# Attention's values computed four heads at a time, one weight piece between key tiles, with the keys' norms tied to the last weight split

## The chip, the cores and the metric

One Trainium2 chip, one core. The metric is the device time of one execution in microseconds (us), the median over runs. Four engines do the work: TensorE (PE), VectorE (DVE), ScalarE (ACT) and GpSimd (POOL). SyncE (SP) issues the DMA transfers that matter here. PE's results land in PSUM, in slots that another engine must empty before they can be used again.

## The reference, cut to what matters

A decoder step of two layers, for 512 prompt tokens and 32 sample tokens at once (544 columns in all), with a width of 1024. After the first layer one shared set of keys and values is made, which is the only part that the change touches:

```python
def shared_kv(h, kv_norm, w_kvf, b_f, k_norm):
    xs = rmsnorm(h, kv_norm)
    kvf = xs @ w_kvf                      # 1024 -> 1024 keys, 1024 values, 8 forget values
    k = rmsnorm(kvf[..., :D_ATT].reshape(bsz, L, N_HEADS, HEAD_DIM), k_norm)
    v = kvf[..., D_ATT:2 * D_ATT].reshape(bsz, L, N_HEADS, HEAD_DIM)
```

There are 8 heads of 128. Keys are normed head by head, values are not. The second layer then begins with its first feed-forward block (called FFN2 here, since it is the second layer's), whose input is prepared while keys and values are still being computed.

## The kernel before, in words

**Precision.** Every fp32 matrix is split into a high part in the rounded matmul format and a low part, the rest. A product takes three matmuls: high by high, high by low, low by high (L241, L245, L247 for keys and feed-forward tiles; L798, L799, L800 for values).

**Weights.** They come in pieces of 128x1024 (512 KB). For each piece SP loads it (L165), ACT casts its high part (L198) and DVE subtracts for the low part (L199). Loads run four pieces ahead of the product that uses them and splits two pieces ahead (`prepare`). Each engine runs its program in order, so a cast or a split that stands behind other work on ACT or DVE comes late whenever that work does.

**A key or feed-forward tile** (`tile_mm`): one piece of weights, 8 blocks of 128 rows, each with three products in two column ranges of 256 and 288: 48 matmuls into one slot of the PSUM pool `ps` (three slots of 128x2x512).

**Keys.** A tile for each head. DVE multiplies the PSUM tile by the tokens' inverse norms (L762), ACT squares it (L708). For four heads at a time, a block of 8 small matmuls with ones sums the squares (L716), ACT and DVE turn the sums into inverse norms (L340 to L347), SP stores four rows (L727), and loads each back spread over 128 partitions (L732). DVE multiplies the key by its row (L860), and the normed key is stored and split (L861, L285, L286). Before the change that multiplication stands behind the last key product, `box["last"]` (L762), in DVE's program, by `issue_after`.

**Values.** Tokens stand on the partitions of the result, so the weights are the moving operand. `v_group` computes two heads at a time: it takes two pieces of weights at once, and for each of four blocks of 128 tokens runs 8 blocks of rows by three matmuls, each 256 columns wide, into a quarter of one `ps` slot. ACT then copies the four quarters out, scaled by the tokens' inverse norms (L804). Sample tokens get 8 small matmuls for each group from the raw weights (L809, into the pool `pb` with two slots of one bank), a scaled copy (L813), and, after the last group, two sums with a constant matrix (L850) that are copied out (L851). Each group's two heads are stored (L816), split (L285, L286) and stored again (L818).

**Beside it.** The input of FFN2 is prepared in pieces: `prep` (ACT L297, DVE L298) for each of 8 blocks and `forms` (ACT L307 and L285, DVE L311 to L314 and L286) for each pair. GpSimd runs a scan for the forget values (L899), and ACT and DVE a few operations on it (L908 and after).

**What sets the order.** `KV_ORDER` is a hand-written list that gives the order in which the steps are issued. A scheduler then places the instructions of each engine; its final order is what the rows below the diff show. Outside the stage of keys and values, the order is the same before and after the change.

## Time and profile before

| what | value |
|---|---|
| median of 3 runs | 2066.95 us (2066.77 to 2067.11) |
| the profiled execution's own time | 2067.01 us |
| its span in the trace | 2065.2 us |
| granted TensorE clock | 1.00 |
| PE busy | 2043.9 us, 99% of the span |
| DVE busy | 1507.2 us, 73% |
| ACT busy | 948.8 us, 46% |
| stage of keys and values: first value matmul | 999.86 us after the span's start |
| last value matmul | 1076.44 us |
| first matmul of FFN2 | 1078.48 us |

The profile is one execution. The span runs from its first to its last recorded work; the execution's own time has 1.8 us around that. Times of instructions are in us from the span's start. PE's rows overlap, since matmuls are pipelined: the cost of a matmul is read from the distance between the starts of consecutive ones, not from its duration.

### The profile page before, as it was taken

How to read it: one execution, taken by the hardware profiler on the slowest of the kernel's cores; microseconds unless marked ns; L12 is line 12 of the kernel's file. 1: busy time of each engine (PE TensorE's matmuls, PEld its weight loads, DVE VectorE, ACT ScalarE, POOL GpSimd, SP SyncE). 2: the span in 40 equal slices, each digit the busy share in tenths (PEclk: the TensorE clock that was granted, in tenths of full speed). 3: DMA queues.
4: the chain of work that ended last, by engine and by line, in shares of the span. 5: the costliest groups of instructions: out<-in, count | busy, mean ns of one | idle time of the engine just before them, and what ended most of it. 6: DMA issues, size and time to landing. Idle time of an engine off the chain costs nothing.

```text
span 2065.2 us, 38837 instructions
## 1 busy us (share of the span) xinstructions
PE 2043.9 (99%) x16432; PEld 2012.3 (97%) x16432; DVE 1507.2 (73%) x1866; ACT 948.8 (46%) x1404; POOL 186.2 (9%) x238
## 2 busy tenths in 40 slices
PE   8999999999999999999999999999999999999999
PEld 8999999999999999999999999999987999999999
DVE  7877777556687777776688777786476888777773
ACT  6535344423554344454356344444364654344451
POOL 0000000400100000043060000001142200000020
PEclk9999999999999999999999999999999999999999
DMA  5233234212223232432374332324668222232421
GB/s 184 84 110 109 73 107 144 94 44 83 83 92 113 72 110 77 151 98 82 115 261 156 105 101 95 113 68 127 208 205 302 102 99 86 100 101 84 131 95 44
DMA packets 93663, 237.95 MB, mean 115 GB/s; under 512 B 9506, under 2 KB 27202, under 8 KB 93490
## 3 DMA queue, kind: packets, MB, share of 16 engines
q1 hardware_dynamic: 93346, 235.44, 34.0%
q8 instruction: 129, 2.11, 0.4%
q14 instruction: 44, 0.36, 0.1%
q10 hardware_dynamic: 144, 0.04, 0.0%
HBM read 218.95 MB, written 16.49 MB: 114 GB/s over the span
## 4 chain that ended last, share of the span: by engine, by line
PE 92%; DVE 3%; ACT 2%; DMA 1%; issue 1%; POOL 0%; SPq 0%; ACTq 0%; DVEq 0%; POOLq 0%
PE ps L491 33%; PE ps L241 16%; PE ps L247 16%; PE ps L245 16%; PE pb L491 5%; DVE big L199 1%; PE ps L1234 1%; DMA tmp<-rows 1%; ACT big L198 1%; PE ps L1238 1%; PE ps L1237 1%; PE ps L1191 0%; DVE big L184 0%; PE ps L798 0%; ACT big L285 0%
## 5 line engine op out<-in xcount | busy, mean ns | idle before, releaser
L491 PE MATMUL ps<-big,big 128*128 128x272 f32 x5616 | 727.7, 288 | 1.7 <-DVE big L508 1.2
L491 PEld LDWEIGHTS ps<-big,big 128*128 128x128 f32 x5616 | 714.3, 188 | 2.3 <-issue 1.6
L199 DVE TENSOR_TENSOR big<-big,big 128x1024 fp32r<-128x1024 f32 (+2 forms) x538 | 592.1, 1103 | 106.7 <-ACT big L198 106.1
L198 ACT CAST big<-big 128x1024 fp32r<-128x1024 f32 (+2 forms) x538 | 487.9, 932 | 267.5 <-DVE big L184 262.7
L241 PE MATMUL ps<-big,big 128*128 128x256 f32 (+1 forms) x2704 | 563.0, 289 | 7.4 <-ACT big L198 7.4
L247 PE MATMUL ps<-big,big 128*128 128x256 f32 (+1 forms) x2704 | 558.7, 288 | 1.3 <-DVE big L199 1.3
L245 PE MATMUL ps<-big,big 128*128 128x256 f32 (+1 forms) x2704 | 558.1, 287 | 0.0
L241 PEld LDWEIGHTS ps<-big,big 128*128 128x128 f32 x2704 | 433.9, 189 | 10.9 <-ACT big L198 7.7
L245 PEld LDWEIGHTS ps<-big,big 128*128 128x128 f32 x2704 | 435.9, 189 | 0.0
L247 PEld LDWEIGHTS ps<-big,big 128*128 128x128 f32 x2704 | 433.1, 188 | 2.9 <-DVE big L199 2.5
L326 POOL TENSOR_TENSOR st<-st,tmp 128x544 f32<-128x544 f32 (+1 forms) x63 | 87.4, 1387 | 1590.6 <-ACT tmp L324 1590.5
L530 DVE SCALAR_TENSOR_TENSOR big<-ps,big 128x544 f32<-128x544 f32 x160 | 115.5, 722 | 106.5 <-PE ps L247 106.4
L184 DVE TENSOR_TENSOR big<-big,big 128x1024 f32<-128x1024 f32 x156 | 190.0, 1218 | 0.0
L499 ACT COPY tmp<-ps 128x544 f32<-128x544 f32 x117 | 71.7, 613 | 141.4 <-PE ps L491 141.4
L454 ACT ACTIVATE big<-big 128x544 f32<-128x544 f32 x88 | 58.0, 660 | 163.2 <-DVE big L451 162.0
L491 PE MATMUL pb<-big,big 128*128 128x272 f32 x936 | 124.0, 288 | 0.0
L451 DVE TENSOR_TENSOR big<-big,st 128x1088 f32<-128x1088 f32 x88 | 113.3, 1290 | 10.6 <-ACT big L513 8.9
L491 PEld LDWEIGHTS pb<-big,big 128*128 128x128 f32 x936 | 120.2, 188 | 0.0
L297 ACT ACTIVATE big<-big,gains 128x544 fp32r<-128x544 f32 (+1 forms) x80 | 55.8, 704 | 118.8 <-DVE big L530 64.9
L286 DVE TENSOR_TENSOR big<-big,big 128x544 fp32r<-128x544 f32 (+1 forms) x112 | 80.9, 728 | 36.3 <-ACT big L285 36.2
L298 DVE SCALAR_TENSOR_TENSOR big<-big,gains,big 128x544 fp32r<-128x544 f32 (+1 forms) x80 | 65.9, 832 | 26.5 <-ACT big L297 26.5
L285 ACT CAST big<-big 128x544 fp32r<-128x544 f32 (+1 forms) x112 | 71.3, 643 | 16.8 <-DVE big L457 8.9
(200 smaller groups left out, 1418.8 us busy)
## 6 DMA issues: line engine op xcount, KB each, us to landing
big<-in_w SPq DMA_DIRECT2D x156, 512.0 KB
big<-in_w2a SPq DMA_DIRECT2D x64, 512.0 KB
big<-in_w2b SPq DMA_DIRECT2D x32, 384.0 KB
big<-in_w13p SPq DMA_DIRECT2D x16, 512.0 KB
big<-in_win SPq DMA_DIRECT2D x16, 512.0 KB
big<-in_wg SPq DMA_DIRECT2D x16, 512.0 KB
big<-in_ck SPq DMA_DIRECT2D x16, 512.0 KB
big<-in_cv SPq DMA_DIRECT2D x16, 512.0 KB
```

The costliest lines, as they stand in the source:

```text
L184: self.nc.vector.tensor_tensor(t, a, b, ALU.add if op == "+" else ALU.subtract)
L198: self.nc.scalar.copy(hi, src)
L199: self.nc.vector.tensor_tensor(lo, src, hi.bitcast(F32), ALU.subtract)
L241: i = nc.tensor.matmul(out[:, a:b], wh, xh[:, a:b], start=s, stop=False)
L245: nc.tensor.matmul(out[:, a:b], wh, xl[:, a:b], start=False, stop=False)
L247: nc.tensor.matmul(out[:, a:b], wl, xh[:, a:b], start=False, stop=e)
L286: self.nc.vector.tensor_tensor(pair[:, 1, cols], src, pair[:, 0, cols].bitcast(F32), ALU.subtract)
L326: nc.gpsimd.tensor_tensor(acc[:, cols], acc[:, cols], sq, ALU.add)
L451: tt(g, g, rstd.unsqueeze(1).broadcast_to([P, 2, T]), ALU.mult)
L491: nc.tensor.matmul(dst[w], a[:, c], b, start=k in "152" and kp == 0 and n == 0, stop=kp == NKP - 1 and n == 2, skip_group_check=True)
L499: nc.scalar.copy(t["r" + k], t["C" if k == "5" else "A"])
L530: nc.vector.scalar_tensor_tensor(h[c], whole(out), 0.5, h[c], ALU.mult, ALU.add)
```

## The change

The values are computed in 8 steps of one piece of weights each. `_moving` lays the pieces out on the host so that one holds 512 columns (four heads) of two blocks of rows. Four steps make a half of the heads; two `ps` slots are held through the four steps (`half["p"]`), one for each pair of token blocks. A step has 24 matmuls of 512 columns. The sample tokens' products follow steps 1 and 3 of a half, four at a time, 512 columns wide. After the fourth step ACT empties both slots with 8 copies of 128x256 (now L829) and the sample's slot with one (L832). The step `w` stores and splits two heads; a half has two of them. The order list is written anew; value steps now stand between the later key tiles, so the weights' order changes too. Key norms stand behind `last_lo`, the last weight split (L199) that had been issued on DVE, where they stood behind the last key product.

The core of the diff (long unchanged or merely renamed parts left out; `columns`, `raw_sample` and `sample_sums` are the former inner code as methods):

```diff
-:k0|:k1|c|:k2|:k3|v0:,s0,,r0 r1|:k4 n0 r2|:k5 n1 r3|:k6 n2|:k7 n3|v1:,s1,p0,r4 r5 p1|v2:n4 p2,r6,n5 p3 f0,r7 p4|v3:n6 p5 f1,n7,p6,p7
+k0 k1 c0 k2 k3 k4 s0 k5 r0 r1 v0 k6 n0 r2 k7 n1 r3 p0 v1 n2 s1 p1 v2 n3 p2 v3 r4 r5 p3 f0 v4 n4 r6 w0 p4
+v5 n5 r7 w0 p5 v6 n6 f1 p6 v7 n7 p7 w0 w0
...
-        self.nc.vector.tensor_tensor(lo, src, hi.bitcast(F32), ALU.subtract)
+        self.last_lo = self.nc.vector.tensor_tensor(lo, src, hi.bitcast(F32), ALU.subtract)
...
+    def token_half(self, xs, xraw, half, u):
+        nc = self.nc
+        hi, lo = self.unit()
+        raw = self.raws[self.pieces[self.p_next - 1]["src"][0]]
+        self.advance()
+        if u == 0:
+            half["p"] = self.ps(), self.ps()
+            half["r"] = []
+        half["r"] += [raw[:, 0:512], raw[:, 512:1024]]
+        for i in range(4):
+            t, out = slice(i * P, i * P + P), half["p"][i // 2][:, i % 2, :]
+            for a in range(2):
+                k, c = 2 * u + a, slice(512 * a, 512 * a + 512)
+                xh, xl = xs[k]
+                nc.tensor.matmul(out, xh[:, t], hi[:, c], start=k == 0, stop=False)
+                nc.tensor.matmul(out, xh[:, t], lo[:, c], start=False, stop=False)
+                nc.tensor.matmul(out, xl[:, t], hi[:, c], start=False, stop=k == NC_ - 1)
+        if u % 2:
+            if u == 1:
+                half["s"] = self.pb()
+            for n in range(4):
+                k = 2 * u - 2 + n
+                nc.tensor.matmul(half["s"][32 * n:32 * n + 32, :], xraw[:, k, :], half["r"][k], start=k < 4, stop=k >= 4,
+                                 skip_group_check=True)
...
-        def v_group(g, beside):
+        def v_step(n):
+            g, u = divmod(n, 4)
+            self.token_half(xs, xraw, half, u)
+            if u < 3:
+                return
             rc = box["rc"]
...
+            vs = [self.flat(1024).rearrange("p (h i d) -> p h i d", h=2, i=4) for _ in range(2)]
             for i in range(4):
...
+                for a in range(2):
+                    nc.scalar.activation(
+                        vs[a][:, :, i], half["p"][i // 2][:, i % 2, 256 * a:256 * a + 256].rearrange(
+                            "p (h d) -> p h d", h=2), AF.Copy, scale=rc[:, i:i + 1])
+            nc.scalar.activation(sv[:, 512 * g:512 * g + 512], half["s"], AF.Copy, scale=rc[:, 4:5])
...
+        def v_store(_):
+            for hh, x in box["v"][:2]:
+                pair = self.big(F32R)
+                nc.sync.dma_start(out=o["v"][hh], in_=x)
                 self.split_pair(pair, x, slice(0, SEQ))
+                nc.sync.dma_start(out=self.vd[hh], in_=pair[:, :, :SEQ].bitcast(F32))
...
         def norm(hh):
-            with self.tc.issue_after(box["last"].ins):
+            with self.tc.issue_after(self.last_lo.ins):
                 self.k_norm(hh, kraw, rows)
...
+def _moving(w):
+    return w.reshape(4, 2, P, -1, 512).transpose(3, 0, 2, 1, 4).reshape(-1, P, 1024)
...
-    a["wv"] = w_kvf[:, D:2 * D].reshape(2, 4, P, 4, 256).transpose(3, 0, 2, 1, 4).reshape(8, P, 1024)
+    a["wk"], a["wv"] = _stationary(w_kvf[:, :D]), _moving(w_kvf[:, D:2 * D])
```

How the rows of the engines' programs move is shown at three places. In the names, a buffer is its pool and a number; `ps_12037` is the PSUM slot of before's last value group, `ps_11746` and `ps_11747` are the two of after's second half, and the line numbers of after are its own (L603 to L605 for L798 to L800, L611 for L809, L617 for L850, L829 for L804, L832 for L813, L868 for L851).

PE's program of before where the values end:

```order
L798 MATMUL ps_12037<-big_11845,big_10841 128x256
L799 MATMUL ps_12037<-big_11846,big_10841 128x256
L800 MATMUL ps_12037<-big_11845,big_10841 128x256
L809 MATMUL pb_12203<-big_11670,xraw 32x256 x4
L809 MATMUL pb_12203<-big_11676,xraw 32x256 x4
L850 MATMUL pb_12224<-big_11362,consts 32x512
L241 MATMUL ps_12253<-big_11781,big_12025 128x256
L241 MATMUL ps_12253<-big_11781,big_12025 128x288
```

PE's program of after, between the sixth and the seventh of the eight value steps:

```order
L605 MATMUL ps_11747<-big_11664,big_10601 128x512
L611 MATMUL pb_11828<-big_11472,xraw 32x512 x2
L611 MATMUL pb_11828<-big_11554,xraw 32x512 x2
L611 MATMUL pb_11828<-big_11625,xraw 32x512 x2
L611 MATMUL pb_11828<-big_11668,xraw 32x512 x2
L617 MATMUL pb_12012<-big_10940,consts 32x512
L603 MATMUL ps_11746<-big_11733,big_10700 128x512
L603 MATMUL ps_11747<-big_11733,big_10700 128x512
L617 MATMUL pb_12015<-big_10940,consts 32x512
L604 MATMUL ps_11746<-big_11734,big_10700 128x512
```

The sample's products of the last heads and their two sums stood between the last value matmul and FFN2 (the second sum inside FFN2's first tile). They now stand ahead of the last 46 value matmuls, and FFN2's first tile follows the last value matmul directly.

ACT's program of before around the third group's sample copy (L813), which PE's products of that group release:

```order
L198 CAST big_11845<-big_11676 128x1024
L285 CAST big_11887<-big_11431 128x512
L297 ACTIVATE big_11891<-big_87,gains 128x544
L285 CAST big_11951<-big_11431 128x512
L297 ACTIVATE big_11955<-big_87,gains 128x544
L307 ACTIVATE big_11958<-big_86,gains 128x544 x2
L813 ACTIVATE big_11362<-pb_12005,sm_11082 128x256
L285 CAST big_11963<-tmp_11961 128x544
```

ACT's program of after around the second half's sample copy (L832):

```order
L198 CAST big_11733<-big_11625 128x1024
L832 ACTIVATE big_10940<-pb_11828,sm_11083 128x512
L285 CAST big_11775<-big_11263 128x512
L285 CAST big_11781<-big_11701 128x512
L285 CAST big_11786<-big_11701 128x512
L297 ACTIVATE big_11791<-big_88,gains 128x544
L198 CAST big_11794<-big_11668 128x1024
L285 CAST big_11836<-big_11263 128x512
L285 CAST big_11842<-big_11702 128x512
L285 CAST big_11847<-big_11702 128x512
L297 ACTIVATE big_11852<-big_88,gains 128x544
L198 CAST big_11855<-big_11737 128x1024
```

Of before, the copy stands behind casts and preparations that belong to earlier work. Of after, it stands ahead of the casts of the first half's heads (`big_11701`, `big_11702`) and of the casts of three weight pieces, which all wait in ACT's program until PE has done that sample block.

ACT's program of before from the last group's copies to the weight cast of FFN2's third tile (`big_12247`):

```order
L804 ACTIVATE big_12038<-ps_12037,sm_11082 128x2x128 x4
L285 CAST big_12213<-big_12038 128x512
L285 CAST big_12218<-big_12038 128x512
L851 COPY big_12223<-pb_12224 32x512
L851 COPY big_12223<-pb_12227 32x512
L307 ACTIVATE big_12233<-big_88,gains 128x544 x2
L285 CAST big_12238<-tmp_12236 128x544
L285 CAST big_12239<-tmp_12237 128x544
L198 CAST big_12247<-big_12029 128x1024
```

ACT's program of after at the same place, from behind the eight copies L829 to the weight cast of FFN2's third tile (`big_12035`):

```order
L285 CAST big_11984<-big_11455 128x512
L297 ACTIVATE big_11988<-big_89,gains 128x544
L285 CAST big_11991<-big_11970 128x512
L285 CAST big_11996<-big_11970 128x512
L285 CAST big_12001<-big_11971 128x512
L285 CAST big_12006<-big_11971 128x512
L868 COPY big_12011<-pb_12012 32x512
L868 COPY big_12011<-pb_12015 32x512
L307 ACTIVATE big_12021<-big_88,gains 128x544 x2
L285 CAST big_12026<-tmp_12024 128x544
L285 CAST big_12027<-tmp_12025 128x544
L198 CAST big_12035<-big_11859 128x1024
```

Where four copies and two casts of heads stood ahead of the rest, eight copies, four casts of heads, the cast of the last key and one more preparation now stand.

More of the change, by code (lines that the diff above doesn't have):

```diff
@@ L565, in next_norm, with raw_sample, columns, sample_sums @@
         return on_chunk, box
+    def raw_sample(self, h, gcol, x):
+        for c in range(NC_):
+            self.nc.gpsimd.tensor_scalar(x[:, c, :], h[c][:, SEQ:], self.gain(gcol + c), None, ALU.mult)
+        return x
+    def columns(self, rstd):
+        nc, t = self.nc, self.pb()
+        for j in range(4):
+            nc.tensor.matmul(t[:, j:j + 1], rstd[:, j * P:(j + 1) * P], self.ident[:, 0:1], start=True, stop=True)
+        for j in range(4):
+            nc.tensor.matmul(t[32 * j:32 * j + 32, 4:5], rstd[:, SEQ:], self.ident[:, 0:1], start=True, stop=True,
+                             skip_group_check=True)
+        rc = self.sm(5)
+        nc.scalar.copy(rc, t[:, 0:5])
+        return rc
+    def token_half(self, xs, xraw, half, u):
[21 more added lines that the diff above has]
+                nc.tensor.matmul(half["s"][32 * n:32 * n + 32, :], xraw[:, k, :], half["r"][k], start=k < 4, stop=k >= 4,
+                                 skip_group_check=True)
+    def sample_sums(self, sv, half):
+        t = self.pb()[:NS, :]
+        self.nc.tensor.matmul(t, self.c[:, C_SUM:C_SUM + NS], sv[:, 512 * half:512 * half + 512], start=True, stop=True)
+        return t
     def pairs(self, box):
@@ L750, in kv @@
         nxt = {"x": {}, "f": []}
-        box = {}
+        box, half, sv = {}, {}, self.flat(1024)
         xraw = self.small.tile([P, NC_ * NS], F32, tag="xraw", name="xraw", bufs=1)[:].rearrange("p (c t) -> p c t", t=NS)
-        for c in range(NC_):
-            nc.gpsimd.tensor_scalar(xraw[:, c, :], h[c][:, SEQ:], self.gain(G_KV + c), None, ALU.mult)
+        self.raw_sample(h, G_KV, xraw)
         def k_tile(hh):
@@ L831, in prep, with forms @@
             nxt["x"][c] = self.prep(h[c], ffn_gain + c)
-        def forms(_):
-            nxt["f"].append(self.forms(h, ffn_gain, len(nxt["f"]), self.pairs(nxt)))
-        do = dict(k=k_tile, s=stats, r=row, n=norm, p=prep, f=forms)
-        parse = lambda s: [[lambda x=x: do[x[0]](int(x[1])) for x in y.split()] for y in s.split(",")]
-        for step in KV_ORDER:
-            head, _, rest = step.partition(":")
-            if head == "c":
-                columns()
-            elif head:
-                v_group(int(head[1]), parse(rest))
-            else:
-                for run in parse(rest)[0]:
-                    run()
+        def forms(n):
+            nxt["f"].append(self.forms(h, ffn_gain, n, self.pairs(nxt)))
+        do = dict(k=k_tile, v=v_step, w=v_store, c=cols, s=stats, r=row, n=norm, p=prep, f=forms)
+        for step in KV_ORDER.split():
+            do[step[0]](int(step[1:]))
         vs = self.big()[:NS, :, :512]
         for a in range(2):
-            t = self.pb()
-            nc.tensor.matmul(t[:NS, :], self.c[:, C_SUM:C_SUM + NS], box["sv"][:, 512 * a:512 * a + 512], start=True, stop=True)
-            nc.scalar.copy(vs[:, a, :], t[:NS, :])
+            nc.scalar.copy(vs[:, a, :], self.sample_sums(sv, a))
         nc.sync.dma_start(out=o["vs"].rearrange("t (a n) -> t a n", a=2), in_=vs)
@@ L1285, in build @@
         ple_units(0)
-        plain([i["wf"]] + [i["wk"][c] for c in range(4)] + [i["wv"][c] for c in range(2)])
-        plain([i["wk"][c] for c in range(4, 8)] + [i["wv"][c] for c in range(2, 8)])
+        plain([i["wf"]] + [i["w" + x[0]][int(x[1])] for x in KV_ORDER.split() if x[0] in "kv"])
         self.ffn_pieces(2)
```

51 lines of the change are left out of this document (5 added, 46 removed).

## The prediction

> **What bounds the kernel now.** I read the page first: busy times, then the chain of work that ended last.
>
> ```profile
> PE 2043.9 (99%) x16432; PEld 2012.3 (97%) x16432; DVE 1507.2 (73%) x1866; ACT 948.8 (46%) x1404; POOL 186.2 (9%) x238
> PE 92%; DVE 3%; ACT 2%; DMA 1%; issue 1%; POOL 0%; SPq 0%; ACTq 0%; DVEq 0%; POOLq 0%
> ```
>
> TensorE is busy 99% of the span and holds 92% of the chain. So the change can act in two ways only: by PE work that goes or comes, and by waits of PE that go or come. Then I cut the stage of the values out by windows. The columns are the stretch, its length, busy time and count of PE, weight loads, DVE, ACT and POOL, granted clock, DMA share and GB/s.
>
> ```profile
> 999.86:1076.44 76.58, 76.58 (x658) 72.31 (x656) 60.40 (x78) 35.93 (x60) 34.16 (x35) 1.00 0.64 219
> 1076.44:1105.20 28.76, 28.00 (x217) 25.23 (x216) 23.53 (x32) 21.40 (x35) 0.30 (x1) 1.00 0.81 281
> ```
>
> From the first value matmul to the last, PE never stops: 76.58 of 76.58. Nothing can be won there but PE's own work. After it PE is short by some 0.8 us, and ACT, at 21.40 of 28.76, and DVE, at 23.53, are far busier than their averages over the span: the preparation of FFN2 piles up here. PE's timeline shows where it stops.
>
> ```profile
> 1076.64 1.07 PE L809 MATMUL pb<-big,xraw 128*32 128x256 f32 x16
> 1077.53 1.02 PE L850 MATMUL pb<-big,consts 128*32 128x512 f32 x2
> 1078.48 0.52 PE L241 MATMUL ps<-big,big 128*128 128x256 f32 x2
> ...
> 1091.77 0.41 PE L241 MATMUL ps<-big,big 128*128 128x256 f32 x2
> ...
> 1092.72 0.52 PE L247 MATMUL ps<-big,big 128*128 128x256 f32 x2 [0.30 <-DVE big L199]
> ...
> 1098.57 0.42 PE L245 MATMUL ps<-big,big 128*128 128x256 f32 x2
> 1099.45 0.52 PE L247 MATMUL ps<-big,big 128*128 128x256 f32 x2 [0.46 <-DVE big L199]
> ```
>
> FFN2 begins at 1078.48; I call that moment P0. Its third tile begins at 1091.77, 13.3 us later. Of that, 1.1 is the second sum (0.95 from 1077.53 to 1078.48 for the first one, and 0.1 for entering), so a tile takes (13.3 - 1.1)/2 = 6.1. Pairs of one line follow at 0.25, so L247 of the third tile was due at 1091.77 + 0.50 = 1092.27 and came at 1092.72: 0.45 late, on DVE's split. In the fourth tile it was due at 1098.57 + 0.25 and came 0.63 late. Together 1.1 us: that is all that PE waits there now.
>
> **Part one: PE's own work.** The value matmuls of before and, from the attention of the second layer, a train of 512-wide ones:
>
> ```profile
> 999.86 0.28 PE L798 MATMUL ps<-big,big 128*128 128x256 f32 x1
> ...
> 1005.45 0.28 PE L800 MATMUL ps<-big,big 128*128 128x256 f32 x1
> ...
> 1509.84 0.39 PE L1076 MATMUL ps<-big,big 128*128 128x512 f32 x1
> ...
> 1510.54 0.28 PE L1082 MATMUL ps<-neg,identr 128*128 128x256 f32 x1
> ```
>
> From 999.86 to 1005.45 lie 47 steps: 0.119 us for a matmul of 256 columns, 384 x 0.119 = 45.7 us. From 1509.84 to 1510.54 lie three of 512 columns: 0.233 each, 192 x 0.2325 = 44.6. Halving the number and doubling the width saves 1.1 us and no more, since the columns set the time.
>
> One rule speaks against that size. The Trainium skill, "TensorE: Matmul & The Clock Gate", section "Back-to-back issue gap", gives about 131 ns as the sustained spacing of 512-wide matmuls; by it the 192 would take an estimated 25.2 us. The trace's 0.233 does not agree, and it decides.
>
> Sample products: four blocks now, each 1.00 from the rows below plus 0.2 for entering and leaving, 4.8 us.
>
> ```profile
> 1012.62 1.07 PE L809 MATMUL pb<-big,xraw 128*32 128x256 f32 x16
> 1013.62 0.52 PE L241 MATMUL ps<-big,big 128*128 128x256 f32 x2
> ...
> 1039.47 0.65 PE L716 MATMUL pb<-tmp,ones 128*32 128x272 f32 x2
> 1040.05 0.39 PE L799 MATMUL ps<-big,big 128*128 128x256 f32 x1
> ...
> 1044.41 1.12 PE L716 MATMUL pb<-tmp,ones 128*32 128x272 f32 x14
> 1045.46 0.39 PE L798 MATMUL ps<-big,big 128*128 128x256 f32 x1
> ```
>
> After, there are two blocks of twice the width: 2 x (2.00 + 0.2) = 4.4, so -0.4 (between 0, if entering doubles too, and -0.6). The second statistics (L716) stood as one matmul alone and seven together: 0.58 + 1.05 and twice the entering, 1.8. After, two stand inside the sample block and three times some stand between value matmuls: 2 x 0.07 + 2 x 0.68 + 1.0 = 2.5, so +0.7 (0 to +1). The two sums only move. Net: -1.1 - 0.4 + 0.7 = -0.8, and with the ends of these terms -1.7 to 0. I take -1.1, nearer the good end, since the long trains of 512 also spare entries that I have not counted.
>
> The second sum now waits for the sample's copy (L832), with 1.1 of the first sum and two value matmuls, 0.5, between. The copy is 0.6 by the casts of the same size below, so I cost it at nothing; if ACT comes to it late, each us past 1.6 is a us of PE.
>
> **Part two: what ACT and DVE owe FFN2.** This is the term that decides. Groups of ACT's instructions, from 1057 to 1100 (busy us and mean ns after the bar), then a window of ACT alone, then its timeline and DVE's split:
>
> ```profile
> L198 ACT CAST big<-big 128x1024 fp32r<-128x1024 f32 x6 | 6.1, 1045 | 0.0
> L307 ACT ACTIVATE big<-big,gains 128x544 f32<-128x544 f32 x8 | 5.5, 737 | 0.0
> L285 ACT CAST big<-tmp 128x544 fp32r<-128x544 f32 x8 | 5.2, 648 | 6.5 <-DVE tmp L311 5.2 <-DVE tmp L314 1.3
> L285 ACT CAST big<-big 128x512 fp32r<-128x512 f32 x8 | 4.8, 618 | 2.4 <-DVE big L860 2.2
> L297 ACT ACTIVATE big<-big,gains 128x544 fp32r<-128x544 f32 x6 | 4.4, 745 | 0.0
> L804 ACT ACTIVATE big<-ps,sm 128x256 f32<-128x256 f32 x8 | 3.1, 463 | 0.0
> ```
> ```profile
> 1057.50:1083.10 25.60, 18.11 (x30) 1.00 0.96 337
> ```
> ```profile
> 1083.11 1.54 ACT L804 ACTIVATE big<-ps,sm 128x256 f32<-128x256 f32 x4
> ...
> 1090.37 1.05 ACT L198 CAST big<-big 128x1024 fp32r<-128x1024 f32 x1
> ```
> ```profile
> 1091.44 1.23 DVE L199 TENSOR_TENSOR big<-big,big 128x1024 fp32r<-128x1024 f32 x1 [0.23 <-ACT big L198]
> ```
>
> Prices, busy over count: weight cast 1.02, L307 0.69, cast of a form 0.65, cast of a head 0.60, L297 0.73, value copy 0.39.
>
> Before, ACT reached the last value copies at 1083.11, ended the third tile's cast at 1091.42, and so took 8.3 us from the one to the other. After, in that piece of ACT's program stand four more value copies (+1.56), three more casts of heads or keys (+1.8) and one more L297 (+0.73): 8.3 + 4.1 = 12.4.
>
> When does ACT reach it? Its program holds the second half's sample copy ahead of everything else that is due, and PE reaches the end of that sample block 48 value matmuls and two sums before P0: 48 x 0.2325 + 2.2 = 13.4 us. From there to the value copies stand one copy (0.6), seven casts of heads and keys (4.2), three L297 (2.2), three weight casts (3.06), two L307 (1.38) and two casts of forms (1.3): 12.7 us of work. ACT works hand in hand with DVE there, so it waits. In the like stretch of before it was busy 18.11 of 25.60, 71%; without some 2 us that DVE lost beside GpSimd's scan, which after comes earlier, 77%. So 12.7 takes 16.5 to 17.9, and the value copies begin at P0 + 3.1 to P0 + 4.5. The third tile's cast ends at P0 + 15.5 to P0 + 16.9. The third tile is wanted at P0 + 12.2, two tiles after P0, as the sums no longer stand between. It starts 3.3 to 4.7 late, and L247 waits for DVE's split (1.23, of which the first two lines cover 0.5) another 0.7: 4.0 to 5.4. Without any wait of ACT the cast ends at P0 + 11.7 and only L247 is some 0.2 late. Between these ends I take 4.2, close to the rows with waits, on their lower side as ACT has less to ask of DVE while its own list is longer. The fourth tile keeps its 0.6. So PE waits 4.8 where it waited 1.1: **+3.7**.
>
> **Parts that I cost at nothing.** The keys move between value steps; their products are the same number. Weights come in another order, but still four pieces ahead, under a DMA share of 0.64 in the stage. Norms behind `last_lo`: the order on DVE then is split first, norm second, so a late row no longer holds that split; the cover is two pieces ahead, and what it costs if that is gone is the rival on rows below.
>
> **Sum**, against the profiled execution's 2067.01 (0.06 above the median, which changes nothing): 2067.0 - 1.1 + 3.7 = **2069.6 us**. That is slower by 0.13%; a measurement of this kernel can tell about 0.2%, 4.1 us, from no change.
>
> **The rivals.**
>
> *ACT keeps up.* If ACT and DVE hardly wait for each other, PE's stalls come to 0.2 + 0.6 = 0.8 for 1.1 now: 2067.0 - 1.1 - 0.3 = 2065.6. For it: ACT has only 25 us of work from the sample copy to the cast, in 25.6. Against it: in the two stretches quoted ACT was busy 71% and 74%.
>
> *Rows of the last keys land late* (the side of slower). The second statistics' rows are stored, loaded back, and used by a multiplication on DVE, behind which weight splits stand. Before:
>
> ```profile
> 1051.53 1.12 SPq L727 DMA_DIRECT2D rows<-st  x4
> 1053.08 0.84 SPq L816 DMA_DIRECT2D out_v<-big  x2
> ```
> ```profile
> 1059.00 1.31 DVE L860 SCALAR_TENSOR_TENSOR big<-big,gains,tmp 128x544 f32<-128x544 f32 x1 [0.42 <-DMA tmp<-rows]
> ```
>
> From the end of the statistics (1045.46) to the row in use (1059.00) 13.5 us went by, 7.5 of them in stores, loads and queue. After, the last statistics stand 31 value matmuls, the sample block, the sums and 48 value matmuls ahead of P0: 7.2 + 2.2 + 2.2 + 11.2 = 22.8. The last value step, wanted at P0 - 5.6, has its split on DVE behind the first such multiplication, three splits of heads and a few more, 1.3 + 3 x 0.65 + 1.4 + 1.2 = 5.9. So a row may land 11.3 us after the statistics; each us beyond is one of PE's. Four stores of values (1 MB) now stand directly ahead of the rows in SP's queue where two stood between store and load. With the 13.5 of before PE loses 2.2 more in the value steps: 2071.8. For it: that row. Against it: 6.1 of the 13.5 were DVE's own queue, beside a scan that is earlier now.
>
> *PSUM.* A half holds two of three `ps` slots, so a key tile inside it must use the third, and the next key tile waits until DVE has emptied it. If DVE is 4 us behind there, this costs some 3.5 us: 2073. Against it: only one key tile stands inside a half's steps after the first, and PE's windows show DVE busy 60 of 77.
>
> *The width costs nothing.* If a matmul cost 0.119 whatever its width, 192 x 0.119 = 22.8 would go: 2067.0 - 22.8 + 3.7 = 2048. The 0.233 of L1076 speaks against it. By the 131 ns of the Trainium skill's page "TensorE: Matmul & The Clock Gate", section "Back-to-back issue gap", it would be an estimated 2050.
>
> *The change doesn't save at all.* If the new trains break at each block as short ones do, the saving of 1.1 is nil: 2070.7; this lies within the forecast's own spread.
>
> **How the numbers follow.** Forecast with its spread (2068.6 to 2070.8): 0.56. ACT keeps up: 0.18. Rows late: 0.16. PSUM: 0.05. Width free: 0.02. The rest, 0.03, is something unseen, either way. The low end is the case in which ACT keeps up, 2065.4; the high end, 2072.7, takes in late rows with 0.9 us over. Faster by over 0.2% (below 2062.8): the width rival and half of the unseen, with a little of ACT keeping up and PE saving more, 0.06. Slower by over 0.2% (above 2071.1): late rows, PSUM and a little more, 0.22. Within: 0.72.
>
> **What would show it.** Right: in the profile after, 512-wide value matmuls at 0.233; the third FFN2 tile's first product waiting some 3.5 us for ACT's weight cast, that cast ending near P0 + 16, ACT's value copies starting near P0 + 4; nothing else of PE's waits in the stage. Wrong: a spacing far from 0.233; ACT's copies starting at P0 or before, or the third tile on time; PE waiting inside the value steps on a weight split (rows late: DVE's multiplication waits for the DMA) or on DVE's key product (PSUM).

## The result, and the profile after

The kernel after takes 2071.60 us (median of 13 runs, 2070.17 to 2072.89) where the kernel before, run beside it, takes 2066.77 (13 runs). The ratio is 1.0026, with a 95% interval of 1.0019 to 1.0033: slower by about a quarter of a per cent. The forecast was 2069.6, within 2065.4 to 2072.7. The profiled execution took 2071.60, 4.6 us more than the one of before. Of the experiments below, three executions in a slow state (3202.8 us of e1_old_tie, 2841.93 of e6_gpsimd_cast, 4049.92 of e10_values_earlier) are left out of the medians and ratios, while one of 2087.45 us of e8_late_cast is in them and lifts its ratio to 1.0034, where the medians alone give 1.0026.

The page of after, the engines' busy times:

```profile
PE 2044.9 (99%) x16208; PEld 2003.2 (97%) x16208; DVE 1507.3 (73%) x1866; ACT 948.2 (46%) x1402; POOL 181.4 (9%) x238
```

PE has 224 matmuls fewer (192 of the values and 32 of the sample, half the number at twice the width), and yet it is busy 1 us longer. Windows of after, from the first value matmul to FFN2, from there to FFN2's first matmul of the next kind (L491), and a piece of the latter (columns as in the prediction; the granted clock stands third from the end):

```profile
1012.38:1077.62 65.24, 65.24 (x343) 49.73 (x341) 53.64 (x69) 28.27 (x46) 28.78 (x34) 1.00 0.59 200
1077.62:1109.77 32.15, 27.86 (x194) 26.90 (x193) 24.88 (x33) 23.83 (x39) 0.21 (x1) 0.89 0.92 334
1094.57:1101.17 6.60, 6.60 (x28) 6.29 (x28) 5.83 (x8) 6.28 (x9) 0.00 (x0) 0.50 0.97 313
```

In the value steps PE never waits, as before. Behind them it stands still for 4.3 us, and for 6.6 us of its work the clock is granted at 0.50. PE's timeline of after shows the order of events:

```profile
1075.07 0.40 PE L604 MATMUL ps<-big,big 128*128 128x512 f32 x1
...
1077.38 0.40 PE L605 MATMUL ps<-big,big 128*128 128x512 f32 x1
1077.62 0.41 PE L241 MATMUL ps<-big,big 128*128 128x256 f32 x2
...
1082.77 0.52 PE L245 MATMUL ps<-big,big 128*128 128x256 f32 x2 [0.26 <-DVE big L298]
1083.13 0.41 PE L247 MATMUL ps<-big,big 128*128 128x256 f32 x2
1084.35 0.52 PE L241 MATMUL ps<-big,big 128*128 128x256 f32 x2 [0.82 <-ACT big L829]
...
1090.95 0.41 PE L247 MATMUL ps<-big,big 128*128 128x256 f32 x2
1094.57 0.82 PE L241 MATMUL ps<-big,big 128*128 128x256 f32 x2 [3.21 <-ACT big L198]
1095.19 0.66 PE L245 MATMUL ps<-big,big 128*128 128x256 f32 x2
...
1101.31 0.41 PE L247 MATMUL ps<-big,big 128*128 128x256 f32 x2
...
1109.77 0.65 PE L491 MATMUL ps<-big,big 128*128 128x272 f32 x4
```

Matmuls of 512 columns follow at (1077.38 - 1075.07)/10 = 0.231. P0 is 1077.62. Measured by how much later than its regular distance a start comes, PE waits 0.42 for DVE's L298, 0.97 until ACT's copies L829 free a PSUM slot for the second tile, and 3.38 for the weight cast of the third tile: 4.78 in all, against 1.08 before. Behind the last wait a pair of matmuls takes 0.45 instead of 0.25 until about 1101.2.

A stretch that holds all of this can be closed by four rows. It begins with the first L241 behind the block of L491 that ends at 872, some 100 us ahead of the keys; from there to the keys the order is the same in both kernels. It ends with the first L491 of FFN2 (1109.77 above). The text calls it the stage. Before:

```profile
872.17 0.42 PE L241 MATMUL ps<-big,big 128*128 128x256 f32 x2
...
1105.04 0.53 PE L491 MATMUL ps<-big,big 128*128 128x272 f32 x3
```

After:

```profile
871.48 0.42 PE L241 MATMUL ps<-big,big 128*128 128x256 f32 x2
```

That is 232.87 before and 238.29 after: +5.42. Up to P0, the second sum of before counted with it (1.11: two tiles take 13.29 with it and, after, 12.18 without), PE needs 206.31 + 1.11 = 207.42 before and 206.14 after: -1.28. The waits add 4.78 - 1.08 = 3.70. From the third tile's start to L491 it is 15.20 after and 13.27 - 1.08 = 12.19 before: the slow clock costs 3.01. The sum is -1.28 + 3.70 + 3.01 = +5.43. The rest of the 4.6 lies outside: the stage begins 0.69 earlier, in a part that is the same in both kernels, and some 0.1 is gained behind it.

Why is the cast late? ACT's timeline of after, and the multiplication of the first late key on DVE:

```profile
1064.54 0.69 ACT L832 ACTIVATE big<-pb,sm 128x512 f32<-128x512 f32 x1 [1.57 <-PE pb L611]
...
1071.70 1.66 ACT L285 CAST big<-big 128x512 fp32r<-128x512 f32 x3 [3.33 <-DVE big L877]
...
1082.74 3.02 ACT L829 ACTIVATE big<-ps,sm 128x256 f32<-128x256 f32 x8
...
1093.48 1.04 ACT L198 CAST big<-big 128x1024 fp32r<-128x1024 f32 x1
```
```profile
1064.15 0.78 DVE L877 SCALAR_TENSOR_TENSOR big<-big,gains,tmp 128x544 f32<-128x544 f32 x1
```

The third tile's weight cast itself (1093.48) waits for nothing: it starts when ACT is through with what stands ahead of it, so the load of the weights is not what makes it late. Earlier, ACT is held up by PE at the sample copy and by DVE at the key casts. Groups of ACT's waits from 1000 us on show the second of these; the line is that of before (up to 1092), then that of after (up to 1096):

```profile
ACT big L285 <- DVE big L860: 3.1, 3, 1.2
```
```profile
ACT big L285 <- DVE big L877: 17.9, 6, 5.7
```

And from 975 us to P0, ACT and DVE have done less by then (fourth and third of the busy times; before, then after):

```profile
975.00:1078.48 103.48, 103.48 (x882) 97.84 (x880) 77.28 (x99) 49.21 (x77) 34.69 (x36) 1.00 0.49 169
```
```profile
975.00:1077.62 102.62, 102.62 (x655) 86.29 (x653) 73.45 (x95) 43.33 (x67) 28.78 (x34) 1.00 0.40 138
```

ACT is 5.9 us behind at P0 and DVE 3.8, though neither has more to do in the whole run (948.2 against 948.8, and 1507.3 against 1507.2). The work was put off until after the values, and FFN2 asks for it.

### The profile page after: what moved, and what is told of

It reads as the page before. It is cut to its first block, busy times and chain, and to the rows that moved or that the text cites. A ratio compares the mean times of both kernels' runs of the same rounds, so it can differ in the third digit from the quotient of the medians.

```text
span 2069.8 us, 38397 instructions
## 1 busy us (share of the span) xinstructions
PE 2044.9 (99%) x16208; PEld 2003.2 (97%) x16208; DVE 1507.3 (73%) x1866; ACT 948.2 (46%) x1402; POOL 181.4 (9%) x238
## 4 chain that ended last, share of the span: by engine, by line
PE 91%; DVE 4%; ACT 2%; issue 1%; DMA 1%; POOL 0%; SPq 0%; ACTq 0%; DVEq 0%; POOLq 0%
PE ps L491 33%; PE ps L241 16%; PE ps L247 16%; PE ps L245 16%; PE pb L491 5%; DVE big L199 1%; PE ps L1251 1%; PE ps L1255 1%; PE ps L1254 1%; ACT big L198 1%; ACT big L285 0%; PE ps L1208 0%; DVE big L286 0%; DVE big L184 0%; DMA tmp<-rows 0%
## 5 line engine op out<-in xcount | busy, mean ns | idle before, releaser
L491 PE MATMUL ps<-big,big 128*128 128x272 f32 x5616 | 727.7, 288 | 1.7 <-DVE big L508 1.2
L491 PEld LDWEIGHTS ps<-big,big 128*128 128x128 f32 x5616 | 714.2, 188 | 2.3 <-issue 1.6
L199 DVE TENSOR_TENSOR big<-big,big 128x1024 fp32r<-128x1024 f32 (+2 forms) x538 | 593.2, 1105 | 108.3 <-ACT big L198 107.4
L241 PE MATMUL ps<-big,big 128*128 128x256 f32 (+1 forms) x2704 | 564.5, 290 | 11.1 <-ACT big L198 10.3
L241 PEld LDWEIGHTS ps<-big,big 128*128 128x128 f32 x2704 | 434.7, 189 | 14.2 <-ACT big L198 11.0
L491 PE MATMUL pb<-big,big 128*128 128x272 f32 x936 | 124.0, 288 | 0.0
L491 PEld LDWEIGHTS pb<-big,big 128*128 128x128 f32 x936 | 120.2, 188 | 0.0
L298 DVE SCALAR_TENSOR_TENSOR big<-big,gains,big 128x544 fp32r<-128x544 f32 (+1 forms) x80 | 67.4, 848 | 27.0 <-ACT big L297 27.0
L285 ACT CAST big<-big 128x544 fp32r<-128x544 f32 (+1 forms) x112 | 71.0, 644 | 31.6 <-DVE big L877 17.9
```

What stands on the lines that cost most here:

```text
L199: self.last_lo = self.nc.vector.tensor_tensor(lo, src, hi.bitcast(F32), ALU.subtract)
L241: i = nc.tensor.matmul(out[:, a:b], wh, xh[:, a:b], start=s, stop=False)
L491: nc.tensor.matmul(dst[w], a[:, c], b, start=k in "152" and kp == 0 and n == 0, stop=kp == NKP - 1 and n == 2, skip_group_check=True)
```

## The experiments

Each was timed in five rounds beside the kernel before. "Stage" is the distance from the first matmul at 872 to the first L491 of FFN2, as above, less that of before; waits of PE (over 0.4 us, from the last value matmul on, by the starts of its rows) and stretches at half clock (as the trace's record of the granted clock has them) are from each run's one profile. The kernel before had medians of 2066.31 us beside e1 to e4, 2066.27 beside e5 to e8, 2066.16 beside e9 and e10 and 2065.74 beside e11 and e12, so medians of different rounds compare to about 1 us.

| run | median us | ratio to before (95%) | stage | PE's waits | half clock |
|---|---|---|---|---|---|
| after | 2071.60 | 1.0026 (1.0019 to 1.0033) | +5.4 | 0.42, 0.97, 3.38 | 6.8 |
| e1_old_tie | 2072.76 | 1.0030 (1.0019 to 1.0042) | +6.6 | 3.37, 0.65 | 3.4 |
| e2_early_splits | 2070.43 | 1.0020 (1.0011 to 1.0029) | +0.2 | 0.43, 0.97, then six of 0.65 to 1.06 from the first L491 on | none |
| e3_filler | 2070.97 | 1.0022 (1.0013 to 1.0032) | +3.8 | 0.46, 0.97, 0.51, 0.65, 0.64 | none |
| e4_before_tie | 2069.09 | 1.0015 (1.0006 to 1.0023) | +2.1 | 2.58, 0.65, 0.65 | none |
| e5_gpsimd_splits | 2075.63 | 1.0044 (1.0031 to 1.0057) | +8.5 | 1.67, 0.47, 0.97, 3.94, 1.19 | 6.8 |
| e6_gpsimd_cast | 2071.44 | 1.0022 (1.0012 to 1.0032) | +5.1 | 0.46, 0.97, 2.31, 0.58 | 6.8 |
| e7_before_gpsimd | 2070.86 | 1.0023 (1.0014 to 1.0032) | +3.8 | 3.27 | 3.4 |
| e8_late_cast | 2071.55 | 1.0034 (1.0020 to 1.0047) | +4.9 | 4.10, 0.66 | 3.4 |
| e9_no_late_casts | 2068.39 | 1.0013 (1.0004 to 1.0022) | +2.5 | 0.42, 0.97, 1.30, 0.65 | 3.4 |
| e10_values_earlier | 2072.00 | 1.0029 (1.0018 to 1.0040) | +5.2 | 2.99, 2.22, 0.65, 0.65 | 3.4 |
| e11_old_order | 2069.49 | 1.0017 (1.0008 to 1.0026) | +2.6 | 3.09, 0.52 | 3.4 |
| e12_old_order_early | 2067.77 | 1.0011 (1.0002 to 1.0020) | +2.2 | 2.53, 0.65 | 3.4 |

The theory: values four heads at a time, woven between the keys, put ACT and DVE behind by P0; FFN2's third tile then waits for its weight cast, and behind a wait of that length the chip halves the clock. Rivals: the tie of the norms does it; the slow clock has a cause of its own; moved work simply comes back elsewhere.

### The clock: e3_filler and e8_late_cast

After, with matmuls that nobody reads in the place where PE waits:

```diff
+                if lead and gcol == G_FFN1 + 8 and f == 1 and w == 0:
+                    t = self.pb()
+                    for j in range(24):
+                        self.tc.keep_in_program_order(
+                            nc.tensor.matmul(t[:, :256], self.last_w, xs[0][0][:, :256], start=True, stop=True))
```

> The kernel after, with 24 extra matmuls of 256 columns (2.9 us at 0.119 each, result unused) on PE between FFN2's second and third tile, where PE waits 3.4 us. They stand in the wait and take nothing off ACT's lateness. Theory (PE standing still for over 3 us is what halves the granted clock for the next 6.5 us): the third tile starts at the same moment, the clock stays at 1.00, and the time falls by the 3.0 us that the slow clock cost: 2068.6. Rival (the slow clock has another cause, such as the load of the long 512-wide trains ahead of it): the clock falls just the same, 2071 to 2072.

PE's timeline of this run at the third tile, and its window behind it:

```profile
1091.54 3.03 PE L427 MATMUL pb<-big,big 128*128 128x256 f32 x24
1094.92 0.52 PE L241 MATMUL ps<-big,big 128*128 128x256 f32 x2 [0.34 <-ACT big L198]
...
1096.18 0.52 PE L247 MATMUL ps<-big,big 128*128 128x256 f32 x2 [0.48 <-DVE big L199]
```
```profile
1095.00:1103.00 8.00, 7.04 (x53) 1.00 0.99 341
```

The third tile starts as late as ever, and the clock stays at 1.00: standing still, not the trains ahead, lowers it. In the stage this brings 1.6 us, not 3.0, since two waits for DVE's split (0.65 and 0.64) that the slow tile had hidden come out. Of the median only 0.6 is left, and 0.2 by the distance from the kernel before of its own round; the 2068.6 of the theory was missed. In this profile the second layer's attention took 1.5 us longer (240.5 from FFN2's last L491 to the next block's first, 238.9 in after); why, and whether other executions lose the gain there too, is not shown. So the mechanism is shown; the price of the slow clock is 3.0 gross and 1.6 net in the stage, and of that the median of this run shows hardly any.

The other half of the test, the kernel before with its value matmuls untouched and one weight cast run five times:

```diff
-        self.nc.scalar.copy(hi, src)
+        for _ in range(5 if self.p_split == self.late else 1):
+            self.nc.scalar.copy(hi, src)
...
+        self.late = len(self.pieces) + 2
         self.ffn_pieces(2)
```

> The kernel before, its value matmuls untouched, with the weight cast of FFN2's third tile run five times over (four more of 0.95 us each into the same buffer), so that it ends at 1095.2 instead of 1091.4 while PE wants it at 1091.8. Theory (a wait of over about 3 us alone makes the chip grant half the clock for some 6 us): PE waits 3.4 us, then the clock falls to 0.50 for about 6 us, costing 3 more: 2066.3 + 3.4 - 0.4 + 3.0 = 2072, or 1 less where the slow tile hides the waits for DVE. Rival (the slow clock needs the long trains of 512 ahead of it): 2069.3, clock at 1.00.

```profile
1094.94 0.52 PE L242 MATMUL ps<-big,big 128*128 128x256 f32 x2 [3.94 <-ACT big L199]
...
1096.20 0.82 PE L248 MATMUL ps<-big,big 128*128 128x256 f32 x2 [0.50 <-DVE big L200]
1096.82 0.66 PE L242 MATMUL ps<-big,big 128*128 128x256 f32 x2
...
1099.09 0.41 PE L248 MATMUL ps<-big,big 128*128 128x256 f32 x2
```

(The lines are one further than in before.) One late cast is enough: the clock is halved from 1095.7 to 1099.1, about half as long as expected, and the median is 2071.55, for the 2072 or 1 less of the theory. Waits of 4.10 + 0.66 less the 1.08 of before, and some 1.3 for the 2.9 us of PE's work at half clock, make the 4.9 of the stage. No value matmul of 512 columns is in this program, and of that width only four small sums with the constant matrix (L851) stand ahead of the slow stretch.

### The tie: e1_old_tie and e4_before_tie

The tie alone was put back in after, and put alone into before:

```diff
-            with self.tc.issue_after(self.last_lo.ins):
+            with self.tc.issue_after(box["last"].ins):
```

> The new values and the new order, but the key norms stand behind the last key product again. After shows ACT waiting 5.3 us for the key norms (L877) between 1062 and 1094.5, and the third tile's weight cast ending 3.4 us late. Theory (ACT and DVE hand work back and forth, and the tie to the last split lengthens the chain): ACT's waits for L877 shrink from 5.3 to under 2, the cast of FFN2's third tile comes 2 to 4 us earlier, PE's wait falls under 1.5 us, the clock stays at 1.00: about 2067. Rival (the sum of the work that ACT and DVE do there sets the time, DVE 26.4 of 32.0 us): the cast comes within 1 us of where it came: 2071 to 2072.

Groups of PE's waits from 990 to 1140, of e1_old_tie:

```profile
PE ps L241 <- ACT big L198: 3.2, 1, 3.2
PE ps L604 <- DVE big L199: 2.2, 2, 1.1
```

ACT's waits for key norms are gone from its list altogether, as the theory said, and yet the cast is as late as it was (3.37 for 3.38), and PE now waits inside the value steps too: norms that stand ahead of the splits hold them until the rows have landed. My theory of the handing back and forth fell here; the rival stood, and the time was worse still than it said.

> The kernel before, with only the key norms' tie moved to the last weight split. Theory (the tie lengthens the chain between ACT and DVE, but before has its tail fixed by four copies and two casts fewer): PE's waits at FFN2's third and fourth tile change by less than 1.5 us, no fall of the clock: 2066 to 2068.5. Rival (the tie alone makes the third tile late): a wait of 3 us or more there with a slow clock behind it, 2070 or above.

```profile
1093.18 0.52 PE L241 MATMUL ps<-big,big 128*128 128x256 f32 x2 [2.42 <-ACT big L198]
...
1094.44 0.52 PE L247 MATMUL ps<-big,big 128*128 128x256 f32 x2 [0.50 <-DVE big L199]
```

In the kernel before, the tie alone makes the third tile 2.58 late and the stage 2.1 longer. The theory had allowed 1.5 of waits and 2068.5; the rival had asked for 3 us, a slow clock and 2070. The measured 2069.09 lies between, and what it says is that the tie has a price of its own, without a slow clock in this profile. The profiled execution (2068.10) is the only one of the eleven with a mean granted clock of 1.000; the others have 0.998 or 0.999, where 23 of the 29 of before beside them have 1.000. So the clock probably fell in most of them, which no profile shows. In the two-by-two of stages, before (0), tie (+2.1), values (+6.6) and both (+5.4), the tie is harmful by itself and worth 1.2 together with the new values, where it spares PE the waits inside the value steps. That last sign rests on one profile each: the intervals of after and e1_old_tie overlap.

### What ACT and DVE owe: e2, e5, e6, e7, e9

Two weight splits of FFN2 issued ahead of the last heads' casts:

```diff
-... v7 n7 p7 w0 w0
+... v7 n7 x0 x0 p7 w0 w0
...
+                  x=lambda _: self._split())
```

> The kernel after, with the weight splits of FFN2's third and fourth tile issued two steps earlier, ahead of the last four heads' casts. Theory (the late cast is the wait, and the wait is what lowers the clock): the third tile's cast ends near 1088 instead of 1094.5, the 3.4 us of waiting and the slow 6.5 us behind it go, the 0.98 wait for the value copies stays: 2071.6 - 3.4 - 3.0 = 2065.2, or up to 1 us more where the 2 us of casts push later work. Rival (ACT and DVE simply have too much to do, and what is done earlier makes something else late): a wait of 2 to 4 us turns up at a later tile, the clock falls there instead: 2070 to 2072.

PE's waits of this run from 1100 to 1130:

```profile
PE ps L491 <- ACT tmp L499: 1.7, 2, 0.9
PE ps L491 <- DVE big L199: 1.0, 2, 0.5
PE ps L491 <- ACT big L198: 0.8, 2, 0.6
```

The third tile was on time, the clock stayed up, and the rival's time came all the same: FFN2's next part, from its first to its last L491, 306.47 us long in before and after alike, took 311.48. The same debt was paid in six small waits, not in the one long one that the rival had named. So the late cast is where the debt shows, not what it is. In after, 6.4 us of waiting and slow clock gave ACT and DVE the time to catch up.

Then the debt was made smaller. The values' splits for the second layer went to GpSimd (in e6 only the casts; in e7 the kernel before):

```diff
-                self.split_pair(pair, x, slice(0, SEQ))
+                nc.gpsimd.tensor_copy(pair[:, 0, :SEQ], x)
+                nc.gpsimd.tensor_tensor(pair[:, 1, :SEQ], x, pair[:, 0, :SEQ].bitcast(F32), ALU.subtract)
```

> The kernel after, with the values' casts and splits for the second layer (per head one cast and one subtraction of 128x512) on GpSimd instead of ACT and DVE. GpSimd is idle there (0.21 of 16.2 us). That takes four casts of 0.6 and four subtractions of 0.62 out of the last stretch, and as many out of the steps before. Theory (ACT and DVE are behind by their sum of work, and PE pays for it): the third tile's cast comes 2.2 to 4.4 us earlier, PE's wait falls from 3.4 to at most 1.2 and the clock stays at 1.00: 2065.5 to 2068. Rival (GpSimd slows DVE beside it, as DVE's L347 took 1.69 beside the scan and 0.72 without): DVE loses what ACT gains, the third tile stays late by 3 us or more: 2070 to 2073.

> The kernel after, with only the values' casts on GpSimd; the subtractions stay on DVE. Tells ACT's share of the lateness from DVE's. If ACT's list sets the third tile's cast: nearly the gain of moving both, 2066 to 2068.5. If DVE's does: 2069.5 to 2072.

> The kernel before, with the same casts and splits on GpSimd: the control. If the relief is worth something only where ACT and DVE are behind, before gains at most the 1.1 us that its PE waits at the third and fourth tile: 2065.2 to 2066.5. If it gains as much as the kernel after does (3 us or more, to under 2064), the relief says nothing of the change.

GpSimd's timeline in e5, and PE's only listed wait in e7:

```profile
1087.65 3.24 POOL L840 CAST big<-big 128x512 fp32r<-128x512 f32 x4 [0.39 <-ACT big L829]
1090.86 5.86 POOL L841 TENSOR_TENSOR big<-big,big 128x512 fp32r<-128x512 f32 x4
```
```profile
PE pb L851 <- ACT big L813: 3.2, 1, 3.2
```

GpSimd took 0.8 for a cast and 1.5 for a subtraction, and everything became slower: e5 by 4.0 us against after, e7 by 4.6 against before. The rival of e5 was right in its sign, and the time lay above its range too. In e6 the wait at the third tile falls from 3.38 to 2.31, and the time stays. By its expectation 2071.44 would say that DVE's list sets the cast, but what GpSimd slows is mixed into that time. So moving the work to GpSimd does not answer how much ACT and DVE owe, and e7 is no control for that, only for GpSimd. What it slows, and by which way, these runs do not tell apart.

Leaving work out answers it for ACT and DVE together:

```diff
+                if hh >= 4:
+                    for n in range(2):
+                        nc.sync.dma_start(out=self.vd[hh][:, n], in_=x)
+                    continue
```

> The kernel after, but the values of the last four heads are stored for the second layer unsplit (the same rows twice, by two DMAs): the splitting of these four heads is left out, that is four casts of 0.55 on ACT and four subtractions of 0.62 on DVE, all of them between the last value copies and the third tile's weight cast. Everything ahead of them stays in its order. Theory (ACT and DVE are late by what stands in their lists at the end): the third tile's cast comes 2.2 us earlier, PE's wait there falls from 3.4 to 1.2, the clock stays at 1.00, waits for DVE's split of up to 1.3 come back: 2071.6 - 2.2 - 3.0 + 1.0 = 2067.4. Rival (the cast is late for another reason, such as waiting for the loads of weights or for the value copies alone): the wait stays at 3 us or more, 2071.

ACT's and PE's timeline of this run:

```profile
1091.61 1.04 ACT L198 CAST big<-big 128x1024 fp32r<-128x1024 f32 x1
```
```profile
1092.70 0.52 PE L241 MATMUL ps<-big,big 128*128 128x256 f32 x2 [1.14 <-ACT big L198]
...
1093.96 0.53 PE L247 MATMUL ps<-big,big 128*128 128x256 f32 x2 [0.49 <-DVE big L199]
1094.31 0.63 PE L241 MATMUL ps<-big,big 128*128 128x256 f32 x2
1094.74 0.66 PE L245 MATMUL ps<-big,big 128*128 128x256 f32 x2
```

Four casts fewer on ACT and four subtractions fewer on DVE bring the weight cast 1.9 us forward, PE's wait falls to 1.30, and the median to 2068.39: 3.2 us less than after, or 2.6 by the distance from the kernel before of each round. ACT's share and DVE's are not told apart by it. Theory and measurement agree to 1 us; only the clock did not keep to the bound, since it fell for 3.4 us behind waits of 1.30 and 0.65.

### The order: e10, e11, e12

Only the list of steps is changed, with the tie and the new values kept. e10 has each value step of the first half one key tile earlier:

```diff
+k0 k1 c0 k2 k3 k4 s0 v0 k5 r0 r1 v1 k6 n0 r2 v2 k7 n1 r3 p0 v3 n2 s1 p1
+w0 v4 n3 w0 p2 r4 r5 v5 p3 f0 n4 r6 p4 v6 n5 r7 p5 f1 v7 n6 p6 n7 p7 w0 w0
```

> The kernel after with another order list: each value step of the first half one key tile earlier (v0 ahead of k5, v1 ahead of k6, v2 ahead of k7), the second half's steps without the gap of stores between, so that the first half's copies and casts reach ACT some 10 us earlier and are done before the second half's sample block. Theory (values that come late make ACT and DVE owe work to FFN2): the third tile's wait falls to some 1.3 us, no slow clock, waits for DVE's split at the third and fourth tile come back at 0.7 each: 2071.6 - 2.1 - 3.0 = 2066.5. Rival (the debt does not depend on when the first half is done, only on the four heads that end last): 3 us or more at the third tile, 2071 to 2072.

```profile
PE ps L241 <- ACT big L829: 2.9, 1, 2.9
PE ps L241 <- ACT big L198: 2.1, 1, 2.1
```

This missed: the wait at the third tile fell by 1.2 only, and a new one of 2.99 came at the second tile, for the PSUM slot that the value copies free, because preparations had now moved ahead of the copies. The rival's time came (2072.00), but not by its wait of 3 us at the third tile.

e11 has before's order as nearly as the new steps allow; e12 also has the last preparations one step earlier:

```diff
+k0 k1 c0 k2 k3 v0 s0 v1 v2 r0 r1 v3 k4 n0 r2 w0 k5 n1 r3 w0 k6 n2 k7 n3
+s1 p0 v4 r4 r5 p1 v5 n4 p2 r6 n5 p3 f0 r7 v6 p4 n6 p5 f1 v7 n7 p6 p7 w0 w0
...
+s1 p0 p1 v4 r4 r5 p2 v5 n4 p3 f0 r6 n5 p4 r7 v6 p5 n6 f1 n7 p6 p7 v7 w0 w0
```

> The kernel after with its new value steps and its tie, but in the order of before as nearly as it goes: the first half's four steps together behind k3, then k4 to k7, then the second half. Separates the new width from the new interleaving. Theory (the interleaving with the keys puts ACT and DVE behind, since the heads' stores and the last keys' norms all come in the last third): the waits at FFN2's start fall from 4.8 to some 2.5 in all, no slow clock, and PE's own saving of 1.3 stays: 2066 to 2067.5. Rival (the width itself does it, as a half of four heads ends with eight copies and four casts wherever it stands): 4 us or more of waits and a slow clock, 2070 to 2072.

> The same, with FFN2's last four preparations and its second form one step earlier still, so that only the copies, the casts of heads and one form stand behind the last value matmul. Theory (what stands at the end of ACT's list sets the third tile's cast): 0.3 to 1.5 us faster than the run before it, 2065.5 to 2067. Rival (moved work comes back as a wait elsewhere, as in the run with early splits): within 0.5 us of the run before it, or slower.

PE's waits, of e11 and of e12:

```profile
PE ps L241 <- ACT big L198: 2.9, 1, 2.9
```
```profile
PE ps L241 <- ACT big L198: 2.4, 1, 2.4
```

Without the interleaving the waits are 3.6 for 4.78 and the stage +2.6 for +5.4, but the cast is still 3.09 late and the clock still falls. Neither side had the size: 2069.49 lies between the theory's 2066 to 2067.5 and the rival's 2070 and above, nearer the rival. So in these profiles the interleaving accounts for about half of the loss. The other half need not come from the halves of four heads: the tie alone cost 2.1 in the order of before (e4_before_tie), which leaves them 0.5, and the order of before with the new values and without the tie was not run. e12, with less behind the last values, is another 1.7 us faster, a little more than the 0.3 to 1.5 of its theory, though not within its 2065.5 to 2067. At 2067.77 it is the best of the versions with the new values that compute everything, and still 1.0011 times before: none beats it.

## Why the prediction was right and where it was wrong

**PE's own work, -1.1.** Right: -1.28. The matmul of 512 columns was taken at 0.233 and has 0.231, so the width alone saves 45.7 - 192 x 0.231 = 1.3; the sample blocks and statistics, put at +0.3, came to about nothing, which is not shown term by term. The Trainium skill's 131 ns ("TensorE: Matmul & The Clock Gate", "Back-to-back issue gap") does not hold for these matmuls in either kernel.

**What ACT and DVE owe FFN2, +3.7.** Right in its mechanism, and in sum, 3.70, by luck: the two forecast waits of 4.2 and 0.6 came to 1.4 less, and two waits that no step had named made up 1.39. ACT's value copies were forecast at P0 + 3.1 to 4.5 and began at P0 + 5.1 (1082.74); from there to the cast's end it took 11.8 (forecast 12.4), so that the cast ended at P0 + 16.9, the late end of the range given. The third tile lost 3.38, not 4.2, and the fourth nothing, not 0.6: the slow clock covered the two waits for DVE's split, as e3_filler showed by bringing them back. In their place came 0.97 for the PSUM slot and 0.42 for L298.

**The missing term.** The step that failed is the sum itself: it turned 4.8 us of waiting into 4.8 us of time. A stop of 3.38 us was followed by 6.6 us at half clock, worth 3.0, and that is the distance of 2.0 from 2069.6 to what was measured, together with 0.7 that the stage began earlier, 0.2 of PE's own work and 0.1 behind the stage that went the other way. e3_filler took the slow clock away without touching the wait, e8_late_cast made it in the kernel before. Without it the kernel would not have come to 2069.6 all the same: e3_filler has 2070.97, since waits come out that the slow clock had hidden. The prediction read the granted clock of before, 1.00 all through, as a constant, but the longest stop of PE in that stage had been 0.63 us, and the forecast one was 4.2. The Trainium skill, "TensorE: Matmul & The Clock Gate", section "Part 1: The HAM clock gate", says that PE falls to half rate after an idle window of about 3.4 us, and that the windows run freely. These runs agree with the half rate (0.50) and with windows of that length (the clock changes in steps of 3.41 us), but a window need not be idle throughout: in the one ahead of the slow stretch of e9_no_late_casts PE was busy for 1.78 us. The last section has the numbers.

**The parts at nothing.** The tie was not free: +2.1 us in the stage of before by itself (e4_before_tie, where ACT's waits for key norms rise from 3.1 to 15.2 us), and -1.2 with the new values (e1_old_tie against after, one profile each). The cover that I named, splits two pieces ahead, is what it protects within the value steps; that it uses the cover up at the end is inferred, not shown.

**The rivals.** ACT did not keep up. The rows of the last keys were in time: DVE's first multiplication of a late key, at 1064.15, waited for nothing. No key tile waited for PSUM; the wait for a slot came at FFN2's second tile, and in e10_values_earlier it was the largest of that run. The width is not free.

**The sides.** The chance for slower by over 0.2% was 0.22. The measured 0.26% lies beyond that line, and its interval includes the line. With a term of 3 us for the clock the same working would have given 2072.6 and put most of the chance on slower. The measured 2071.60 lies above the forecast's own spread (2068.6 to 2070.8). It lies within the whole range only because the high end, 2072.7, was set for late rows, which did not come: that it held is luck.

**What stays open.** Why ACT is 5.9 us behind at P0 is shown only in part: it waits 17.9 us for key norms in after, but e1_old_tie took those waits away and the cast was no earlier. The waits had moved to DVE's side and into the value steps. Which of the orders that the scheduler could make would leave no debt was not found in three tries.

## What to carry to other kernels

Where one engine is busy 99% of the time, price not only how long it will wait, but whether the wait is long enough to lower its clock: here one stop of 3.4 us cost 3 us more, of which 1.6 us were left in the stage once the later waits that the slow clock had hidden came out. When work of a side engine is put off, look at what the bound engine asks of it next, and compare how much of the work is done by that moment, before and after. A wait that is moved by issuing one step earlier is not a debt paid: e2_early_splits shows the sum coming back in FFN2's next part.

## What the runs showed of the hardware

**How long a stop lowers the clock.** All seven stops of about 3 us and more (2.99 to 4.10, in seven profiles) were followed by half clock. Of four between 2.2 and 2.6, two were (e6_gpsimd_cast, e12_old_order_early) and two were not (e4_before_tie, the second one of e10_values_earlier). One of 1.30 with 0.65 behind it was (e9_no_late_casts). Before, e2 and e3, with no single stop over 1.06, never fell in this stage. What parts the shorter ones is in the traces' records of the granted clock: it changes only at the ends of steps of 3.41 us that run on through the whole profile (in after it first falls 317 steps, 1082.03 us, behind the record's start), and each slow stretch lasts one step (3.41) or two (6.83). The stop of 2.53 in e12 falls into one step, the one of 2.58 in e4 is divided between two. The windows show two steps of each, e12 first (stretch, length, busy time and count of PE, granted clock, DMA share, GB/s):

```profile
1089.18:1092.59 3.41, 1.04 (x8) 1.00 1.02 347
1092.59:1096.00 3.41, 3.00 (x14) 0.50 0.95 337
```
```profile
1089.04:1092.45 3.41, 1.72 (x14) 1.00 1.01 351
1092.45:1095.86 3.41, 2.19 (x15) 1.00 1.01 333
```

Over all steps of the fourteen profiles, from full clock, every one in which PE was busy for 1.46 us or less was followed by a slow step, and none in which it was busy for 1.80 or more. Between these lie five, of which only one was (e9, 1.78). PE's ends are modelled, so the line can't be drawn more finely than about half a step. Where the steps lie in the program differs from profile to profile (their record starts 10.2 to 13.8 us after the span's start), so the same stop of some 2 to 2.6 us can lower the clock in one execution and not in another. Why the slow stretch lasted two steps in after, e5 and e6 and one in the others is not shown.

**GpSimd beside DVE.** A cast of 128x512 to the rounded format took 0.6 to 0.9 on GpSimd and 0.60 on ACT; the subtraction took 1.5 to 2.0 on GpSimd and 0.62 on DVE. Sixteen such instructions there in place of ACT and DVE made the kernel slower by 4 us (e5 against after) and 4.6 us (e7 against before).
